# A two-layer transformer trunk: where the token squares stand, and which engine makes three kinds of product

## The chip, the cores and the metric

The kernel runs on one core of a Trainium2 chip. The metric is the device time of one execution in microseconds (us); lower is better. The core has a matrix engine (TensorE, PE in the rows), a vector engine (VectorE, DVE), a scalar engine (ScalarE, ACT), a general engine (GpSimd, POOL) and a sync engine (SyncE, SP) that issues the DMA transfers. Each works through its own list of instructions in the order in which they stand and waits for the others by semaphores.

## What is computed

The reference runs two layers over 512 tokens of width 1024 in float32. A layer is, cut to what matters here:

```
h = rmsnorm(x, g_pre_mix)
proj = h @ w_in                       # q, k, v, index heads of four attention kinds
mix = concat(attention a, b, c, d)    # q, k of a, d and the index heads take rotary tables
x = x + rmsnorm(mix @ w_out, g_post_mix)
h = rmsnorm(x, g_pre_mlp)
m = square(relu(h @ w_up)) @ w_down
x = x + rmsnorm(m, g_post_mlp)
x = x + sigmoid(x @ w_ple_gate) * (p_i @ w_ple_proj)
```

`rmsnorm(x, g)` is x times the reciprocal root of the mean of its squares over the 1024 columns, times g.

## The kernel before

The 512 tokens are four tiles of 128 (`tt` 0 to 3), and a tile's 1024 columns are two halves of 512. The residual x lies in eight tiles named R (128x512). Every float32 matrix product is made of three matmuls: each operand is split into a rounded part and a rest (`whi`, `wlo` for weights, `hth`, `htl` for the transposed activations). The weights come by DMA into `wst` (two buffers), `whi` is a rounded copy and `wlo` the difference; there are five buffers of each.

**The order of the work** is not written by hand. The builder records all operations, with a priority that is the place of recording (moved by `plan.shift`), and a planner then walks through modelled time with fixed costs and writes out each engine's list. An operation recorded with `plan.either` is given to the engine that the planner finds free sooner. `plan.after(i)` holds recorded operations behind operation i in the planner. A named tile such as X, Z or R has a fixed number of buffers (X 4, Z 6, R 19), which are handed to its users in the order of recording; a later user waits until an earlier one is done.

**A layer's start.** `mixing` multiplies each half tile by the gain (`gained_half`: X <- R, Z), transposes it on TensorE and splits it into `hth`, `htl`. The norm's factor is not applied there: `mean_square` squares both halves on ScalarE (with the sum as a second output, `ss`), two small GpSimd operations make the mean, and a GpSimd power makes column tt of `r`. `row_of` transposes the four columns of r (TensorE), ScalarE copies the row into an X tile, and `rope_tables` multiplies sine and cosine by it, into four tiles `tab`. In layer 0 the tables come from `positions`, which a DMA puts into a Z tile, by some twenty VectorE operations and four sines on ScalarE; in layer 1 they are loaded. The first projections, `ik` and the four `iq`, land in the two PSUM buffers `ps_mm`, and leave them by a shuffle and by a product with a table (R <- ps_mm, tab).

**The output projection** (`token_major` with `evac_w` and `done_w`) goes half by half: half 0 is finished for all four tiles (its products with the gain are P <- P, Z), then half 1 tile by tile: ScalarE squares the tile in PSUM, VectorE multiplies by the gain, GpSimd makes the factor, VectorE adds to the residual (two SCALAR_TENSOR_TENSOR, R <- P, ss, R), and then come, for each half, the product with the MLP's gain (X <- R, Z), four transposes, `hth` and `htl`. The MLP's first two tiles (`cut = 2`) are made in column halves, tokens 0 to 255 first. **The MLP's end and the gate** go the same way; the gate's result is sigmoid(PSUM) times `yq`, added to R (`evac_g`), and written to DRAM.

All planned instructions show line L429, the planner's emitting line, in the profile; so they are told apart by their tiles.

Of the kernel before, what the change touches and what calls it, by code (L numbers as in the profile page):

```python
# [14 lines left out]
ALU = mybir.AluOpType  # L15
# [425 lines left out]
class Builder:  # L441
# [77 lines left out]
    def mean_square(self, x, tt, tag):  # L519

        ss = self.tile([128, 4], F32, "ss")
        with self.plan.after(len(self.plan.ops) - 1):
            for i in range(2):
                self.square_half(ss, x[tt][i], i, tag=tag)
        return ss[:, 3:4]

    def add_normed(self, ss, yg, x):
# [409 lines left out]
    def mixing(self, L, x):  # L937
        nc, t = self.nc, self.t
        lam_init = 0.8 - 0.6 * math.exp(-0.3 * L)
        gb = self.gain(t["g1"][L])  # L940
        hT = self.new_hT()
        self.r = self.const([128, 4], "r")
        self.plan.bias = {"DVE": self.gain_bias}
        for tt, i in [(tt, i) for tt in range(4) for i in (0, 1)] if L == 0 else \
                [(tt, i) for i in (0, 1) for tt in range(4)]:
            with self.plan.shift(self.lead[i] if L else 0):
                self.gained_half(x, gb, tt, i, hT, self.hT_tags[(tt, i)[L == 0] % 2], self.first[2 * tt + i] if L == 0 else "vg")
        for tt in range(4):
            ms = self.mean_square(x, tt, "X")
            nc.gpsimd.tensor_tensor(self.r[:, tt:tt + 1], ms, self.mhalf[:, 0:1], op=ALU.pow)  # L950
        if L == 0:
            self.more_constants()
        with self.plan.shift(self.table_shift):
# [57 lines left out]
        def step_mix():  # L1011
# [11 lines left out]
            a=lambda: self.attention_a(r["aq"], r["ak"], r["va"], r["S"]),  # L1023
            b=lambda: self.attention_b(self.decay(zf), r["bq"], r["bk"], r["vb"]),
# [15 lines left out]
    def layer(self, L, x, last):  # L1040
        nc, t = self.nc, self.t
# [32 lines left out]
        x = self.load_x()  # L1074
        gpost = self.gain(t["g2"][L])
        gb = self.gain(t["g3"][L])
        y = [self.tile([128, D], F32, "P4") for tt in range(4)]
        y = [(a[:, :512], a[:, 512:]) for a in y]
        ss = [self.tile([128, 4], F32, "ss4") for tt in range(4)]
        eps4 = [None] * 4  # L1080
        hT = None

        def evac_w(half, tt, ps):
            if (half, tt) in part:
                z = y[tt][half]
                nc.vector.tensor_tensor(z, ps, part[half, tt], op=ALU.add)
                self.square_half(ss[tt], z, half)
                self.plan.either(*[(e, "tensor_tensor", (z, z, gpost[half]), dict(op=ALU.mult))
                                   for e in ("gpsimd", "vector")])
                return  # L1090
            self.square_half(ss[tt], ps, half)
            nc.vector.tensor_tensor(y[tt][half], ps, gpost[half], op=ALU.mult)

        def done_w(tt):
            nonlocal hT
            if hT is None:
                hT = self.new_hT()
            self.add_normed(ss[tt], y[tt], x[tt])


            for i in range(2):
                self.gained_half(x, gb, tt, i, hT, "ps_sc")
            ms = self.mean_square(x, tt, "Z")
            eps4[tt] = self.tile([128, 1], F32, "eps4")
            nc.gpsimd.tensor_scalar(eps4[tt], ms, ms, EPS, op0=ALU.mult, op1=ALU.mult)

        self.token_major(lambda half, i: t["wo"][L, half, self.mixed[i]], [2 * g + k for g in self.mixed for k in (0, 1)],
                         lambda k: (self.mixh[:, k, :], self.mixl[:, k, :]), evac_w, done_w, (False, True), part)

        self.plan.bias = {"DVE": self.mlp_bias}  # L1110
# [54 lines left out]
        def evac_g(half, tt, ps, c=slice(0, 512)):  # L1165
            s = self.tile([128, T], F32, "Z")[:, c]
            nc.scalar.activation(s, ps, AF.Sigmoid)
            xh = x[tt][half][:, c]
            for o, a, b, op in ((s, s, yq[half, tt][:, c], ALU.mult), (xh, xh, s, ALU.add)):
                self.plan.either(*[(e, "tensor_tensor", (o, a, b), dict(op=op)) for e in ("vector", "gpsimd")])  # L1170
            dst = self.out if last else self.xscr
            nc.sync.dma_start(dst[tt * 128:(tt + 1) * 128, half * 512 + c.start:half * 512 + c.stop], xh)

        self.token_major(lambda half, i: t["wg"][L, half, i], range(8),
                         lambda k: (xT[0][:, k, :], xT[1][:, k, :]), evac_g, lambda tt: None, (True, True), fine=last)
        self.xdram = self.xscr
        return x
# [191 lines left out]
```

## Time and profile before

| | |
|---|---|
| median of three runs | 1526.0 us (1525.25 to 1530.46) |
| the profiled execution | 1525.37 us, of which its span is 1523.4 us |
| TensorE busy | 1443.8 us, 95% of the span |
| VectorE, ScalarE, GpSimd busy | 905.1, 659.9, 405.7 us |
| mean granted TensorE clock | 0.985 |

The span goes from the first to the last instruction; the time of an execution holds some 2 us around it. Busy shares are averages over stages that are limited by different things.

### The profile page before, as it was taken

How to read it: one execution, taken by the hardware profiler on the slowest of the kernel's cores; microseconds unless marked ns; L12 is line 12 of the kernel's file. 1: busy time of each engine (PE TensorE's matmuls, PEld its weight loads, DVE VectorE, ACT ScalarE, POOL GpSimd, SP SyncE). 2: the span in 40 equal slices, each digit the busy share in tenths (PEclk: the TensorE clock that was granted, in tenths of full speed). 3: DMA queues.
4: the chain of work that ended last, by engine and by line, in shares of the span. 5: the costliest groups of instructions: out<-in, count | busy, mean ns of one | idle time of the engine just before them, and what ended most of it. 6: DMA issues, size and time to landing. Idle time of an engine off the chain costs nothing.

```text
span 1523.4 us, 19903 instructions
## 1 busy us (share of the span) xinstructions
PE 1443.8 (95%) x7476; PEld 1171.7 (77%) x7476; DVE 905.1 (59%) x1772; ACT 659.9 (43%) x1298; POOL 405.7 (27%) x309
## 2 busy tenths in 40 slices
PE   6899998998999999999979999889989999999998
PEld 6867777777888888887779678667778888888877
DVE  7789998755424333335555999986554243433463
ACT  4266657644423223233343665667443332322331
POOL 4564455354000000002144636463520000000020
PEclk9899999999999999999999999999999999999999
DMA  4321122223222222221421211113132222222221
GB/s 159 99 84 57 63 77 91 77 83 111 92 88 97 97 97 97 94 88 68 131 92 58 83 56 63 63 63 111 49 125 97 97 98 97 90 90 97 97 74 65
DMA packets 44625, 133.91 MB, mean 88 GB/s; under 512 B 6897, under 2 KB 8177, under 8 KB 44529
## 3 DMA queue, kind: packets, MB, share of 16 engines
q1 hardware_dynamic: 44528, 132.64, 26.4%
q8 instruction: 59, 0.97, 0.3%
q14 instruction: 38, 0.30, 0.1%
HBM read 127.38 MB, written 5.24 MB: 87 GB/s over the span
## 4 chain that ended last, share of the span: by engine, by line
PE 67%; DVE 21%; POOL 4%; issue 3%; ACT 3%; DMA 2%; SPq 0%; ACTq 0%; POOLq 0%; DVEq 0%
PE ps_mm L429 25%; PE ps_sc L429 25%; PE ps_tp L429 16%; DVE Z L429 5%; DVE S L429 4%; DVE R L429 3%; DVE m L429 2%; DVE P L429 2%; PE ps_sc L426 2%; POOL ss L429 2%; DVE O L429 1%; POOL X L429 1%; ACT Z L429 1%; DVE htl L429 1%; DMA wst<-in_wq 1%
## 5 line engine op out<-in xcount | busy, mean ns | idle before, releaser
L429 DVE TENSOR_TENSOR wlo<-wst,whi 128x1024 fp32r<-128x1024 f32 x149 | 188.8, 1268 | 348.9 <-ACT whi L429 348.6
L429 ACT ACTIVATE whi<-wst 128x1024 fp32r<-128x1024 f32 (+1 forms) x210 | 220.4, 1051 | 389.5 <-PE ps_tp L429 204.0
L429 POOL TENSOR_TENSOR wlo<-wst,whi 128x1024 fp32r<-128x1024 f32 (+1 forms) x71 | 171.5, 2418 | 164.3 <-ACT whi L429 155.0
L429 PE MATMUL ps_sc<-hth,wlo 128*128 128x512 f32 (+1 forms) x544 | 208.0, 383 | 0.0
L429 PE MATMUL ps_sc<-hth,whi 128*128 128x512 f32 (+1 forms) x544 | 207.9, 382 | 0.0
L429 PE MATMUL ps_sc<-htl,whi 128*128 128x512 f32 (+1 forms) x544 | 207.5, 382 | 0.0
L429 POOL TENSOR_SCALAR ss<-ss,eps 128x1 f32<-128x1 f32 x8 | 3.8, 477 | 652.3 <-ACT Z L429 652.3
L429 PE MATMUL ps_mm<-hth,whi 128*128 128x512 f32 (+1 forms) x400 | 147.8, 371 | 9.5 <-DVE R L429 8.9
L429 PE MATMUL ps_mm<-htl,whi 128*128 128x512 f32 (+1 forms) x400 | 147.8, 370 | 3.4 <-DVE htl L429 3.4
L429 PE MATMUL ps_mm<-hth,wlo 128*128 128x512 f32 (+1 forms) x400 | 146.1, 366 | 0.9 <-DVE wlo L429 0.9
L429 PE MATMUL ps_mm<-whi,htl 128*128 128x512 f32 (+2 forms) x344 | 120.5, 351 | 5.6 <-DVE htl L429 5.6
L429 PE MATMUL ps_mm<-whi,hth 128*128 128x512 f32 (+2 forms) x344 | 121.4, 353 | 0.4 <-DVE V L429 0.4
L429 PE MATMUL ps_mm<-wlo,hth 128*128 128x512 f32 (+2 forms) x344 | 119.8, 349 | 0.1
L429 PEld LDWEIGHTS ps_sc<-htl,whi 128*128 128x128 f32 x544 | 102.9, 189 | 21.5
L429 PEld LDWEIGHTS ps_sc<-hth,wlo 128*128 128x128 f32 x544 | 102.9, 189 | 21.3
L429 PEld LDWEIGHTS ps_sc<-hth,whi 128*128 128x128 f32 x544 | 103.0, 189 | 21.1
L429 ACT ACTIVATE Z<-Z,m 128x256 f32<-128x256 f32 (+3 forms) x160 | 86.2, 541 | 39.3 <-DVE m L429 38.7
L429 PE MATMUL ps_tp<-whi,V 128*128 128x512 f32 x256 | 96.4, 394 | 0.0
L429 PE MATMUL ps_mm<-whi,V 128*128 128x512 f32 x256 | 96.3, 394 | 0.0
L429 PEld LDWEIGHTS ps_mm<-hth,whi 128*128 128x128 f32 x400 | 78.5, 197 | 20.4 <-issue 11.4
L429 PEld LDWEIGHTS ps_mm<-htl,whi 128*128 128x128 f32 x400 | 78.7, 197 | 14.9 <-DVE htl L429 4.0
L429 POOL TENSOR_TENSOR R<-R,R 128x512 fp32r<-128x512 f32 (+1 forms) x56 | 73.0, 1303 | 57.0 <-ACT R L429 46.8
(214 smaller groups left out, 2978.1 us busy)
## 6 DMA issues: line engine op xcount, KB each, us to landing
wst<-in_wu SPq DMA_DIRECT2D x64, 512.0 KB, 3.2
wst<-in_wd SPq DMA_DIRECT2D x64, 512.0 KB, 3.2
wst<-in_wq SPq DMA_DIRECT2D x40, 512.0 KB, 3.6
wst<-in_wo SPq DMA_DIRECT2D x16, 512.0 KB, 3.2
wst<-in_wg SPq DMA_DIRECT2D x16, 512.0 KB, 3.2
R<-in_x SPq DMA_DIRECT2D x16, 256.0 KB, 3.7
Z<-in_g SPq DMA_DIRECT2D x16, 256.0 KB, 3.3
wst<-in_wv SPq DMA_DIRECT2D x8, 512.0 KB, 3.2
```

The lines of the kernel that those rows point to most:

```text
L426: r = nc.tensor.matmul(*[res(v) for v in a], **k)
L429: r = getattr(getattr(nc, eng), fn)(*[res(v) for v in o.a], **{n: res(v) for n, v in o.k.items()})
```

## The change

Three things are changed. `mean_square` no longer holds its squares behind the operation recorded last. In `mixing` each tile's squares and its column of r are recorded right behind that tile's second gained half, inside its shift, and the squares' unused result goes into a Z tile instead of an X tile. And three kinds of operation that the planner could give to GpSimd or VectorE go to VectorE always: the products P <- P, Z of the output projection's half 0, the products X <- R, Z ahead of the MLP, and the product and sum of the gate.

```diff
     def mean_square(self, x, tt, tag):
         ss = self.tile([128, 4], F32, "ss")
-        with self.plan.after(len(self.plan.ops) - 1):
-            for i in range(2):
-                self.square_half(ss, x[tt][i], i, tag=tag)
+        for i in range(2):
+            self.square_half(ss, x[tt][i], i, tag=tag)
         return ss[:, 3:4]
...
                 self.gained_half(x, gb, tt, i, hT, self.hT_tags[(tt, i)[L == 0] % 2], self.first[2 * tt + i] if L == 0 else "vg")
-        for tt in range(4):
-            ms = self.mean_square(x, tt, "X")
-            nc.gpsimd.tensor_tensor(self.r[:, tt:tt + 1], ms, self.mhalf[:, 0:1], op=ALU.pow)
+
+                if i == 1:
+                    ms = self.mean_square(x, tt, "Z")
+                    nc.gpsimd.tensor_tensor(self.r[:, tt:tt + 1], ms, self.mhalf[:, 0:1], op=ALU.pow)
...
                 self.square_half(ss[tt], z, half)
-                self.plan.either(*[(e, "tensor_tensor", (z, z, gpost[half]), dict(op=ALU.mult))
-                                   for e in ("gpsimd", "vector")])
+                nc.vector.tensor_tensor(z, z, gpost[half], op=ALU.mult)
                 return
...
             for i in range(2):
-                self.gained_half(x, gb, tt, i, hT, "ps_sc")
+                self.gained_half(x, gb, tt, i, hT, "ps_sc", "v")
...
             for o, a, b, op in ((s, s, yq[half, tt][:, c], ALU.mult), (xh, xh, s, ALU.add)):
-                self.plan.either(*[(e, "tensor_tensor", (o, a, b), dict(op=op)) for e in ("vector", "gpsimd")])
+                nc.vector.tensor_tensor(o, a, b, op=op)
```

What this does to the engines' lists follows at three places. Numbers behind a name are a buffer's, and each build numbers anew.

SyncE at the program's start, from the second weight load (wst <- in_wq) on; R <- in_x are halves of tiles 2 and 3, Z <- in_pos the positions. Before:

```order
L429 DMA wst_135<-in_wq 128x1024
L429 DMA Z_140<-in_pos 128x512
L429 DMA invf_147<-in_invf 128x3
L429 DMA R_151<-in_x 128x512
L429 DMA R_155<-in_x 128x512
L429 DMA R_166<-in_x 128x512
L429 DMA R_175<-in_x 128x512
L429 DMA bfb_178<-in_bf 128x4
L429 DMA snk_184<-in_sinks 128x4
L429 DMA wst_205<-in_wq 128x1024
```

After:

```order
L429 DMA wst_142<-in_wq 128x1024
L429 DMA invf_149<-in_invf 128x3
L429 DMA R_156<-in_x 128x512
L429 DMA R_160<-in_x 128x512
L429 DMA R_164<-in_x 128x512
L429 DMA R_175<-in_x 128x512
L429 DMA bfb_184<-in_bf 128x4
L429 DMA snk_190<-in_sinks 128x4
L429 DMA wst_220<-in_wq 128x1024
L429 DMA Z_247<-in_pos 128x512
```

The load of the positions has moved from ahead of x's tiles 2 and 3 to behind the third weight load. On ScalarE in the same stretch the eight squares, which stood behind the last `hth` (two of them behind the first two sines), now stand between the `hth`, ahead of all sines.

ScalarE at layer 1's start, from the last `hth` of the transposed tiles (ps_sc) to the copy of r's row (X <- ps_tp); `X,ss<-R` is a square. Before:

```order
L429 ACTIVATE hth_157<-ps_sc_6850 128x4x128
L429 ACTIVATE X_6883,ss_6884<-R_2911 128x512
L429 ACTIVATE X_6891,ss_6884<-R_2951 128x512
L429 ACTIVATE whi_6903<-wst_6854 128x792
L429 ACTIVATE X_6916,ss_6917<-R_3014 128x512
L429 ACTIVATE X_6926,ss_6917<-R_3099 128x512
L429 ACTIVATE X_6955,ss_6956<-R_3119 128x512
L429 ACTIVATE X_6963,ss_6956<-R_3267 128x512
L429 ACTIVATE whi_6970<-wst_6876 128x792
L429 ACTIVATE X_6976,ss_6977<-R_3272 128x512
L429 ACTIVATE X_6980,ss_6977<-R_3282 128x512
L429 ACTIVATE X_6988<-ps_tp_6930 128x512
```

After (seven of the eight squares stand further up, between the sigmoids and `hth`; the last is `Z_6865,ss_6743<-R_3282`):

```order
L429 ACTIVATE whi_6850<-wst_6807 128x1024
L429 ACTIVATE Z_6865,ss_6743<-R_3282 128x512
L429 ACTIVATE whi_6877<-wst_6826 128x1024
L429 ACTIVATE hth_166<-ps_sc_6881 128x4x128
L429 ACTIVATE whi_6930<-wst_6895 128x792
L429 ACTIVATE X_6959<-ps_tp_6949 128x512
```

No square stands behind a `whi` copy of 792 columns any more.

GpSimd in layer 0's output projection, half 1, from tile 2's power (ss <- ss, mhalf) on. Before:

```order
L429 TENSOR_TENSOR ss_824_3684<-ss_824_3684,mhalf_68 128x1
L429 TENSOR_SCALAR ss_3958<-ss_3958 128x1 x2
L429 TENSOR_TENSOR wlo_3976<-wst_3807,whi_3967 128x1024
L429 TENSOR_SCALAR eps_883_3997<-ss_3958 128x1
L429 TENSOR_TENSOR X_4003<-R_3267,Z_3543 128x512
L429 TENSOR_SCALAR ss_825_3741<-ss_825_3741 128x1
L429 TENSOR_TENSOR ss_825_3741<-ss_825_3741,mhalf_68 128x1
L429 TENSOR_TENSOR X_4050<-R_3272,Z_3536 128x512
L429 TENSOR_SCALAR ss_4055<-ss_4055 128x1
L429 TENSOR_TENSOR X_4081<-R_3282,Z_3543 128x512
```

After:

```order
L429 TENSOR_TENSOR ss_824_3684<-ss_824_3684,mhalf_68 128x1
L429 TENSOR_SCALAR ss_3980<-ss_3980 128x1 x2
L429 TENSOR_SCALAR eps_892_4013<-ss_3980 128x1
L429 TENSOR_SCALAR ss_825_3741<-ss_825_3741 128x1
L429 TENSOR_TENSOR ss_825_3741<-ss_825_3741,mhalf_68 128x1
L429 TENSOR_SCALAR ss_4079<-ss_4079 128x1 x2
L429 TENSOR_SCALAR eps_901_4106<-ss_4079 128x1
```

The 512-column products and the 1024-column subtraction have left GpSimd here; VectorE has them, each X pair right behind its tile's two sums. Over the whole program VectorE has 14 products X <- R, Z, four P <- P, Z and two sums R <- R, Z more, and 17 instructions more in all, since the planner gives it a few others less. Outside the two layer starts and the two passages from the output projection to the MLP, the lists of all engines are the same but for single rows.

## Rows read from the trace of the kernel before

**Rows 1.** The page: span, and busy time with share by engine.

```profile
span 1523.4 us, 19903 instructions
PE 1443.8 (95%) x7476; PEld 1171.7 (77%) x7476; DVE 905.1 (59%) x1772; ACT 659.9 (43%) x1298; POOL 405.7 (27%) x309
```

**Rows 2.** Whom TensorE waited for: us in total, times, longest.

```profile
PE ps_sc L429 <- POOL X L429: 13.5, 13, 3.4
...
PE ps_mm L429 <- DVE R L429: 8.9, 2, 5.1
...
PE ps_tp L429 <- POOL r L429: 7.2, 3, 3.4
```

**Rows 3.** Timeline of TensorE, program start: start, us, [idle before <- releaser].

```profile
38.46 0.47 PE L429 MATMUL ps_tp<-ident,r 128*128 128x128 f32 x1 [3.44 <-POOL r L429]
44.00 0.55 PE L429 MATMUL ps_mm<-hth,whi 128*128 128x256 f32 x1 [5.06 <-DVE R L429]
```

**Rows 4.** Timeline of ScalarE, program start.

```profile
34.68 0.61 ACT L429 ACTIVATE X<-R 128x512 f32<-128x512 f32 x1
...
39.03 0.60 ACT L429 ACTIVATE X<-ps_tp 128x512 f32<-128x512 f32 x1 [1.08 <-PE ps_tp L429]
```

**Rows 5.** Timeline of VectorE, program start.

```profile
22.68 3.24 DVE L429 TENSOR_SCALAR Z<-Z 128x512 f32<-128x512 f32 x3
...
32.48 0.68 DVE L429 SCALAR_TENSOR_TENSOR Z<-Z 128x512 f32<-128x512 f32 x1
```

**Rows 6.** Timeline of GpSimd, program start.

```profile
14.19 6.42 POOL L429 TENSOR_TENSOR X<-R,Z 128x512 f32<-128x512 f32 x4 [1.08 <-DVE wlo L429]
22.97 2.66 POOL L429 TENSOR_TENSOR wlo<-wst,whi 128x1024 fp32r<-128x1024 f32 x1 [2.37 <-ACT whi L429]
```

**Rows 7.** Tile Z, first 40 us: its transfer of positions, the table operations, its transfers' landing.

```profile
L429 DVE TENSOR_SCALAR Z<-Z x10: 408/412/2572, 21.4 to 37.3; 128x512 f32<-128x512 f32 x10
...
L429 SPq DMA_DIRECT2D Z<-in_pos x1: 623/623/623, 6.8 to 6.8; - x1
...
DMA to landing us min/median/max: 2.0/4.5/6.7
```

**Rows 8.** Timeline of TensorE, layer 1's start.

```profile
792.57 0.48 PE L429 MATMUL ps_tp<-ident,r 128*128 128x128 f32 x1 [3.36 <-POOL r L429]
796.88 0.55 PE L429 MATMUL ps_mm<-hth,whi 128*128 128x256 f32 x1 [3.83 <-DVE R L429]
```

**Rows 9.** Timeline of ScalarE, layer 1's start.

```profile
789.83 0.61 ACT L429 ACTIVATE X<-R 128x512 f32<-128x512 f32 x1
...
793.14 0.60 ACT L429 ACTIVATE X<-ps_tp 128x512 f32<-128x512 f32 x1 [2.60 <-PE ps_tp L429]
```

**Rows 10.** Timeline of GpSimd, layer 1's start: tile 3's last sum.

```profile
775.85 1.30 POOL L429 TENSOR_TENSOR R<-R,Z 128x512 f32<-128x512 f32 x1 [22.38 <-PE ps_tp L429]
```

**Rows 11.** TensorE by stretch: length, busy us (matmuls in it), granted clock, DMA share, GB/s.

```profile
798.00:800.00 2.00, 2.00 (x11) 0.50 0.04 8
...
804.00:808.00 4.00, 4.00 (x38) 1.00 0.00 0
```

**Rows 12.** TensorE's waits in 327 to 372 us (first row) and 1080 to 1124 us.

```profile
PE ps_sc L429 <- POOL X L429: 5.0, 5, 3.3
PE ps_sc L429 <- POOL X L429: 6.2, 6, 3.4
```

**Rows 13.** Timeline of TensorE, layer 0's passage from output projection to MLP.

```profile
355.11 0.85 PE L429 MATMUL ps_sc<-ident,X 128*128 128x128 f32 x4 [3.33 <-POOL X L429]
...
369.95 0.39 PE L429 MATMUL ps_sc<-hth,whi 128*128 128x512 f32 x1
```

**Rows 14.** Timeline of GpSimd, same passage.

```profile
350.00 3.35 POOL L429 TENSOR_TENSOR wlo<-wst,whi 128x1024 fp32r<-128x1024 f32 x1
```

**Rows 15.** VectorE's groups: xcount | busy us, mean ns of one | idle before.

```profile
L429 DVE TENSOR_TENSOR wlo<-wst,whi 128x1024 fp32r<-128x1024 f32 x149 | 188.8, 1268 | 348.9 <-ACT whi L429 348.6
...
L429 DVE TENSOR_TENSOR X<-R,Z 128x512 f32<-128x512 f32 x10 | 6.9, 688 | 6.2 <-DMA Z<-in_g 4.9 <-POOL R L429 1.2
```

## The prediction, made before the changed kernel ran

> **What bounds the kernel now.** I read the page first: TensorE is busy for 95% of the span [rows 1], so a change to the other engines can only give back time in which TensorE waits, or runs at the lower of its two clocks. The list of TensorE's waits comes second. Its largest entries are the products X <- R, Z made by GpSimd (13.5 us in 13 waits), the rotary products that empty `ps_mm` (8.9 us in two waits) and the column r (7.2 us in three) [rows 2]. The reader is to see that these 29.6 us are exactly what the change touches, and that each comes at few places. Third I read the timeline at those places, which are four: the start of each layer, and the passage from output projection to MLP in each layer. Since the lists of all engines are otherwise nearly the same before and after, I take every other stretch as unchanged, and the sum has four terms.
>
> **Term A, the program's start: 4.8 us less.** TensorE finishes `ik` and the first `iq` and then stands still for 3.44 us, until the last column of r can be transposed at 38.46, and for 5.06 us more until 44.00, when a rotary product has emptied a `ps_mm` [rows 3]. Two chains end there. One is r: tile 3's squares stand on ScalarE behind the first two sines and begin at 34.68, and the copy of r's row begins at 39.03 [rows 4]. The other is the angles: VectorE's last operation ahead of the first sine runs at 32.48 for 0.68 us [rows 5]. Now r is last, by some 4 us.
>
> In the changed order all squares stand between the `hth`, ahead of the sines. GpSimd's six gain products end near 20.6 (14.19 + 6.42) [rows 6]; with two powers and some means between them and one 2.66 us subtraction [rows 6] behind, r is complete near 26. Then the angles decide, and these come later than before. Their load was issued at 6.84 [rows 7]; now it needs a Z buffer that tile 2's square gives up near 16 (tile 2's gain product begins at 14.19 [rows 6], its square follows an `hth`), and landing takes 2.0 to 6.7 us [rows 7], so 18 to 23. From the conversion of the positions to the product that frees `ps_mm`, VectorE's new list has 27 operations: 12 scalar operations and the conversion at 0.41 [rows 7], eight of 0.68 like the one at 32.48 [rows 5], and six others (two `htl`, two shuffles, two products) that I put at 0.69 like a product of that size [rows 15]. That is 5.3 + 5.4 + 4.1 = 14.9 us. From 20 it ends at 35 if nothing holds it.
>
> Something does. Three of these scalar operations took 3.24 us together [rows 5] while a GpSimd subtraction ran [rows 6], against 1.2 at 0.41 each: 2 us lost to one GpSimd operation. Two such subtractions stand in the stretch after the change, so up to 4 us, and `htl` of tile 3 waits for a product that ends near 21.5. I take 39.2 for TensorE's restart, near the upper end because before, too, the operations beside GpSimd were the long ones: 4.8 us gained. The bounds are 36 (nothing held, 8 us gained) and 42 (positions landed at 23, 2 us gained). A pause of several us remains, so I leave the restart at the lower clock as it is.
>
> The Trainium skill, SBUF — State Buffer, section Who interferes with whom, says that a VectorE operation in a two-port mode, or with two SBUF inputs, and a GpSimd operation that reads SBUF shut each other out for a whole instruction. The 3.24 us agree with that. It speaks against the change, which gives VectorE twenty more operations with two SBUF inputs; it is priced below as the third rival.
>
> **Term C, layer 1's start: 9.5 us less.** Here the tables are loaded early and only r is late. The squares stand on ScalarE behind copies of 792 columns that wait for TensorE; the last begins at 789.83, the copy of r's row at 793.14 [rows 9], and TensorE waits 3.36 us for r and 3.83 for the product that frees `ps_mm`, restarting at 796.88 [rows 8]. From the copy's start to the restart it is 3.74 us. In the new order tile 3's last square follows its last sum, which GpSimd began at 775.85 for 1.30 us [rows 10] and VectorE now makes in 0.69; adding a square of 0.61 [rows 9] and some 2 us of means and power, r is there by 781. TensorE's list has the four transposes of r some 3 us of matmuls ahead of the end of `iq` 0, which came at 788.5 (3.36 + some 0.7 before 792.57 [rows 8]), so the copy begins at 786 and `ps_mm` is free at 786 + 3.74 = 789.8. That is 7.1 us earlier, and leaves a pause of 1 us. After the old pause 11 matmuls fell into 2 us at clock 0.50, against 38 into 4 us at 1.00 [rows 11], that is 19 into 2; the low level held for some 5.5 us, so it cost 5.5 x (1 - 11/19) = 2.3 us. After a pause of 1 us I expect full clock. Sum 9.4, taken as 9.5 with the small wait at tile 3; bounds 7 (the clock falls anyway) and 10.5.
>
> **Terms B and D, the two passages to the MLP: 4.2 us less each.** TensorE waits 5.0 us in layer 0 and 6.2 us in layer 1 for X [rows 12]. The longest wait, 3.33 us up to 355.11 [rows 13], is not for arithmetic but for a queue: tile 2's second X stands on GpSimd behind a subtraction that takes 3.35 us from 350.00 [rows 14]. In the new list VectorE makes X at 0.69 [rows 15] right behind the sums, near 350.6. TensorE's two transposes of tile 2 then stand within the output projection's last matmuls, and the MLP's first column halves begin near 352.5 instead of 355.6. They need 48 matmuls, with tile 3's transposes some 6.5 us (38 fall into 4 us at full clock [rows 11], those that reach over an edge included; I count 34): 359. The second column halves need tile 3. Its square, power, sums, X, and both `hth` and `htl` now stand on VectorE among three `wlo` of 1.27 [rows 15]: counting from tile 3's last matmul near 352.3, 0.8 of square, VectorE's backlog of two `htl` and a `wlo` to 354.5, product 0.7, two sums 1.4, two X 1.3, then `htl`, `wlo`, `htl` behind TensorE's transposes, which gives 361.5. Half of a column half, 1.4 us, hangs on that last `htl`, and one whole follows, 2.8: the first full-width matmul begins at 365.7 against 369.95 [rows 13]. That is 4.2 us. If VectorE's queue costs nothing it is 364.6 and 5.3 us; if each of the three `wlo` takes 2.0 instead of 1.27, it is 2.0. Layer 1 runs the same list, and takes the same.
>
> **What lies under cover.** The four products of half 0 and the gate's two sums stand where TensorE has other tiles' matmuls to run, and VectorE is busy for 59% of the span [rows 1]. At 0.69 each they add 4 us of VectorE work; without cover that would be the cost, and I count nothing.
>
> **Sum.** 4.8 + 9.5 + 2 x 4.2 = 22.7 us off the profiled execution's own 1525.37 us gives **1502.7 us**. The median of the runs, 1526.0, is 0.6 above the profiled one, which is inside what one measurement tells. The bounds together are 13 us (1512.4) and 29 us (1496.3).
>
> **Rivals.**
> First, the positions come too late: if they land behind the third weight load and its copies hold VectorE, the angle chain ends where r did before. Its point of decision is a landing at 25; it speaks for this that the load is now behind the squares and a 512 KB transfer, against it that the transfers pause about there. Term A is then nothing: 1507.5.
> Second, VectorE's queue eats the passages: each X pair stands ahead of a `wlo` and of the next tile's `htl`. For it speaks that VectorE then holds sums, X, `htl` and `wlo` of one tile in one row; against it, that four X pairs at 0.69 add only 5.5 us [rows 15] to a passage of some 40. Terms B and D nothing: 1511.1.
> Third, slower: the moved products meet GpSimd's wide operations and are held for a whole one. One such meeting costs some 2 us (the 3.24 against 1.2), and with 14 X, four P and two sums moved, eleven meetings on a path cancel the gain; sixteen, all those in the passages and the gate, would give 1502.7 + 32 = 1535. Against it: GpSimd's list in the passage has only 1-column operations left between the tiles. By the Trainium skill's rule (SBUF — State Buffer, Who interferes with whom) each meeting would cost what is left of GpSimd's operation.
> A case that the change does nothing, since the squares were not what was waited for, is shut out in layer 1 by the rows; in layer 0 it is the first rival.
>
> **How the numbers follow.** I give the forecast 0.62, the first rival 0.15, the second 0.15, the third 0.04, and 0.04 to unseen waits elsewhere. The predicted time is the forecast's. A range of 1495 to 1512 takes in the bounds of the four terms and both milder rivals, and leaves out the third, the unseen, and part of the others' tails. About 0.5% (7.6 us) is what a measurement of this kernel can tell from no change; faster by more than that means under 1518.4. Forecast and two rivals are under it: faster 0.91, same 0.06, slower 0.03.
>
> **What would show it.** After the change TensorE's waits should hold no X by GpSimd in the passages and next to none for r; in layer 1 it should restart near 790 less the time gained before, at full clock; at the start, r's last transpose should run before the first sine and the restart come near 39, with the last wait on VectorE's table operations. The distance from the output projection's last matmul to the first full-width MLP matmul (18.4 us now) should be near 14. I am wrong if the start restarts after 42, if `htl` of tile 3 holds TensorE for over 3 us, or if a new wait appears in the gate or the attention.

## The result, and where the time went

The changed kernel takes 1507.9 us (median of four runs, 1505.6 to 1514.9) against 1527.0 us for the kernel before on the same chip: a ratio of 0.9878, with a 95% interval of 0.9860 to 0.9896. Its profiled execution took 1507.25 us. The forecast was 1502.7 us with a range of 1495 to 1512: the sign and the range held. The profiled executions, from which the forecast was counted, differ by 18.1 us and the medians by 19.1, where 22.7 us were forecast.

The page of the changed kernel, first lines:

```profile
span 1505.5 us, 19889 instructions
PE 1445.8 (96%) x7476; PEld 1173.3 (78%) x7476; DVE 908.8 (60%) x1789; ACT 661.1 (44%) x1299; POOL 376.7 (25%) x291
```

TensorE is busy for as long as before, GpSimd 29 us less, VectorE 4 us more. TensorE's waits (us in total, times, longest):

```profile
PE ps_mm L429 <- DVE R L429: 9.2, 2, 7.9
...
PE ps_mm L429 <- DVE htl L429: 7.4, 3, 2.8
...
PE ps_sc L429 <- POOL X L429: 2.5, 2, 2.2
```

Of the three entries of [rows 2], X by GpSimd is down from 13.5 to 2.5 us, r is gone, and the rotary product is as large as before: its 7.92 us at the program's start take the place of the 3.44 for r and the 5.06 for the product [rows 3].

**Layer 1's start** is what was forecast. Timelines of TensorE, ScalarE and VectorE there:

```profile
780.00 0.27 PE L429 MATMUL ps_tp<-ident,r 128*128 128x128 f32 x1
784.08 0.36 PE L429 MATMUL ps_mm<-hth,whi 128*128 128x256 f32 x1 [1.31 <-DVE R L429]
...
771.73 0.65 ACT L429 ACTIVATE Z<-R 128x512 f32<-128x512 f32 x1
...
780.31 0.60 ACT L429 ACTIVATE X<-ps_tp 128x512 f32<-128x512 f32 x1 [1.69 <-PE ps_tp L429]
...
783.25 0.68 DVE L429 TENSOR_TENSOR R<-ps_mm,tab 128x512 f32<-128x512 f32 x1
```

The last square now begins 8.6 us ahead of the copy of r's row, r's transposes wait for nothing, and a pause of 1.31 us is left of 3.36 and 3.83 [rows 8]. The granted clock in the stretch behind the pause is 1.00 (19 matmuls in 2 us), where it was 0.50 with 11 [rows 11]:

```profile
786.00:788.00 2.00, 2.00 (x19) 2.00 (x19) 1.98 (x3) 0.63 (x1) 0.76 (x1) 1.00 0.20 29
```

**The passage** from the output projection to the MLP in layer 0, on TensorE: the only wait left, and the first full-width MLP matmul.

```profile
359.75 0.39 PE L429 MATMUL ps_sc<-htl,whi 128*128 128x256 f32 x1 [0.52 <-DVE htl L429]
...
363.54 0.39 PE L429 MATMUL ps_sc<-hth,whi 128*128 128x512 f32 x1
```

**The program's start:** TensorE restarts at 40.83 us, not at 39.2. Timelines of TensorE, then VectorE, then GpSimd:

```profile
40.83 0.55 PE L429 MATMUL ps_mm<-hth,whi 128*128 128x256 f32 x1 [7.92 <-DVE R L429]
...
21.22 0.85 DVE L429 CAST Z<-Z 128x512 f32<-128x512 int32 x1
22.73 3.00 DVE L429 TENSOR_SCALAR Z<-Z,invf 128x512 f32<-128x512 f32 x2
...
29.51 4.67 DVE L429 SCALAR_TENSOR_TENSOR Z<-Z,Z 128x512 f32<-128x512 f32 x4
...
22.83 2.62 POOL L429 TENSOR_TENSOR wlo<-wst,whi 128x1024 fp32r<-128x1024 f32 x1
30.41 2.62 POOL L429 TENSOR_TENSOR wlo<-wst,whi 128x1024 fp32r<-128x1024 f32 x1 [3.60 <-ACT whi L429]
```

r is no longer late; the angle chain begins with the conversion at 21.22 and stands still beside both GpSimd subtractions (two scalar operations 3.00 us, four of the others 4.67).

A ledger shows where the time went. For the same matmul in two traces it gives the start before minus the start after, as a median over a stretch of the kernel before's time; the rise from one column to the next is the gain made between them. It is worked out from TensorE's timelines; the other rows are the experiments below, each by one profiled execution.

```
stretch (us of before)   48-56 180-215 280-300 380-440 680-720 820-850 1060-72 1180-1240 1480-1500
changed kernel            2.3    0.2     1.0     6.3     5.6    14.7    13.8    18.6     18.3
squares_only              3.1    1.0     1.8     3.8     3.1    10.4     7.9     9.8      9.5
products_only             2.4    1.2     1.9     3.1     3.1     3.0     3.1     3.4      3.4
layer0_late               2.5    1.3     2.1     7.4     7.4    17.7    15.4    21.0     21.0
mlp_squares_held          2.5    0.3    -1.9    -1.1    -1.8     7.0     5.4     5.1      4.8
products_low_v            0.3    0.3     1.1     7.5     7.5     6.9     8.1    13.4     13.4
after_low_g               3.6    1.5     2.2     4.0     3.3    11.1     8.5    10.7     10.4
before_hth128             2.4    0.6     0.0    -0.2     0.4    -1.0    -5.1    -5.2     -4.9
r_ss_padded_low_v         2.7    2.5     2.0     9.2     9.4    19.3    18.4    25.2     25.2
```

For the changed kernel: passages 5.3 and 4.8 us (forecast 4.2 each), layer 1's start 9.1 (9.5), and of the program's start (4.8) 1.0 us is left at 280. That is 20.2 us; 1.9 us are lost again in stretches that the forecast took as unchanged (0.7 from 380 to 720, 0.9 from 820 to 1072, 0.3 at the end). So the start is 3.8 us short, the passages are 1.7 us better than forecast, and the losses about cancel that. But why the passages gained was not yet known.

A passage's gain by the ledger takes in the output projection ahead of it. The length of the passage alone, from the output projection's last matmul to the first full-width MLP matmul, fell from 18.6 and 18.4 us (layers 0 and 1) to 13.5 and 13.9.

### The profile page after: what moved, and what is told of

It is laid out like the page before. It is cut to its first block, busy times and chain, and to the rows that moved or that the text cites. A ratio compares the mean times of both kernels' runs of the same rounds, so it can differ in the third digit from the quotient of the medians.

```text
span 1505.5 us, 19889 instructions
## 1 busy us (share of the span) xinstructions
PE 1445.8 (96%) x7476; PEld 1173.3 (78%) x7476; DVE 908.8 (60%) x1789; ACT 661.1 (44%) x1299; POOL 376.7 (25%) x291
## 5 line engine op out<-in xcount | busy, mean ns | idle before, releaser
L429 DVE TENSOR_TENSOR wlo<-wst,whi 128x1024 fp32r<-128x1024 f32 x150 | 184.2, 1228 | 355.6 <-ACT whi L429 355.4
L429 POOL TENSOR_TENSOR R<-R,R 128x512 fp32r<-128x512 f32 (+1 forms) x58 | 76.6, 1321 | 59.1 <-ACT R L429 46.0
```

The costliest lines, as they stand in the source:

```text
L429: r = getattr(getattr(nc, eng), fn)(*[res(v) for v in o.a], **{n: res(v) for n, v in o.k.items()})
```

## The experiments

All times are medians beside the kernel before on the same chip; ratios are to it.

### The parts alone

`squares_only` makes the edits of `mean_square` and `mixing` alone, `products_only` the three others alone (with the squares held and placed as before).

> Only the squares stand early; the three kinds of product stay free between VectorE and GpSimd, as before. Theory (the parts add, each where it stands): layer 1's start gains its 9.5 us, the program's start restarts TensorE near 40.8 and keeps some 1 us of that by 300 us, the two passages stay at 18.4 to 18.6 us from the last output-projection matmul to the first full-width MLP matmul. Sum: 10 to 11 us under the kernel before, some 1515. Rival (layer 1's gain needs the gate's sums on VectorE, since GpSimd's last sum of 1.30 us stands ahead of the last square): layer 1's start gains under 7 us and the sum is under 8 us.

1517.1 us, ratio 0.9945 (0.9929 to 0.9961): 9.1 us, 1 to 2 us less than the theory's sum. Layer 1's start gained 7.3 us (3.1 to 10.4) of the changed kernel's 9.1: most of it comes from the squares. The other 1.8 us go with the edits that are left out here (at 749.65 TensorE waits 1.41 us for an X by GpSimd, 0.26 in the changed kernel); which of them was not run alone. Unforeseen: each passage gained 2 us by the ledger, although no product was moved, and its length alone fell to 14.8 us in both layers, where 18.4 to 18.6 were expected; the output projection ahead took some 1.7 us more. With the squares free the planner gave GpSimd no weight subtraction in these passages; before, one stood in each (layer 0's is in [rows 14]).

> Only the three kinds of product go to VectorE; the squares stand as before. Theory (the parts add): both passages fall to some 13.5 us, 5 us each; the program's start restarts TensorE at 44.0 and layer 1's start still waits over 3 us for r and over 3 us for the rotary product. Sum: 10 us under the kernel before, some 1516. Rival (part of the 10 us in the passages came from what stood ahead of them, not from X on VectorE): under 6 us.

1525.1 us, ratio 0.9989 (0.9977 to 1.0001): next to nothing. The passages gained 1.2 and 0.2 us, not 5, and are 19.1 and 19.8 us long. So the passages' gain is no sum of the parts (2.0 + 1.2 against 5.3). Layer 0's passage in `products_only`, on VectorE, GpSimd and TensorE:

```profile
346.43 3.52 DVE L429 SCALAR_TENSOR_TENSOR R<-P,ss,R 128x512 f32<-128x512 f32 x2
...
346.66 2.74 POOL L429 TENSOR_TENSOR wlo<-wst,whi 128x1024 fp32r<-128x1024 f32 x1 [1.20 <-ACT whi L429]
...
350.70 1.23 PE L429 MATMUL ps_sc<-ident,X 128*128 128x128 f32 x8 [2.50 <-DVE X L429]
```

The planner has left GpSimd two subtractions here. Beside one of them tile 2's two sums take 3.52 us, where two such sums take 1.42 us elsewhere in this passage, and TensorE waits 2.50 us for the X behind them: the third rival's mechanism, in the place where the forecast had ruled it out. The Trainium skill, SBUF — State Buffer, section Who interferes with whom, says that a VectorE instruction with two SBUF inputs contends with a GpSimd instruction that reads SBUF, and that the port pair they share is an exclusive lock. The 3.52 us agree with it.

### The start's part undone, and its load moved

`layer0_late` has the squares of layer 0's start as before; `pos_in_V` lets the positions land in another tile:

```diff
-            posi = self.tile([128, T], I32, "Z")
+            posi = self.tile([128, T], I32, "V")
```

> The change without its part in layer 0's start: there the squares stand at the end as before, in X tiles, and the positions load early. Theory (the start's 3.2 us at the restart are nearly all given back by 120 us: a longer stretch at the low clock after the restart, a slower pace of the matmuls, and a fall of the clock near 115): time within 2.5 us of the changed kernel, 1506 to 1510. Rival (the start's gain is kept, and the loss comes later and from elsewhere): 3 us or more above the changed kernel, 1511 or more.

1506.9 us, ratio 0.9876 (0.9859 to 0.9892), the changed kernel's 0.9878: from the change's part in layer 0's start no gain can be told from noise.

> The change, with the positions landing in a V tile, so that their load waits for no square and stands ahead of x's tiles 2 and 3 as before. Theory (the angle chain on VectorE, from the conversion of the positions on, sets TensorE's restart): the conversion runs near 17 instead of 21.2 and the restart comes 3 to 4 us earlier, at 37 to 38; time 1 to 4 us under the changed kernel, by how much of it the clock gives back. Rival (GpSimd's two 1024-column subtractions and the htl between the angle operations set it, not the start of the chain): restart at 40 or later and the time the same within 1 us.

1507.9 us, ratio 0.9878 (0.9865 to 0.9892): the same, and the theory fell. The conversion ran at 16.76, 4.5 us earlier, but the restart came at 40.72. Single operations of the chain beside GpSimd's subtractions now took 2.83 and 2.40 us, two table products beside a third subtraction 2.92 us together, and `htl` stood between the others. The clock fell in this execution too (0.50 in 29 to 31 us), but VectorE was busy without a pause from the conversion to the product that frees `ps_mm`: its own list and the meetings set the restart, as the rival had it.

Why nothing is left is shown by runs whose lists at the start equal the kernel before's word for word on all engines. Granted clock of TensorE in 27 to 31 us, first the kernel before, then `products_only` (length, busy us, matmuls, clock, DMA share, GB/s):

```profile
27.00:29.00 2.00, 2.00 (x15) 0.69 0.55 221
29.00:31.00 2.00, 2.00 (x11) 0.50 0.00 0
```

```profile
27.00:29.00 2.00, 2.00 (x20) 1.00 0.47 188
29.00:31.00 2.00, 2.00 (x19) 1.00 0.00 0
```

```profile
41.98 0.55 PE L429 MATMUL ps_mm<-hth,whi 128*128 128x256 f32 x1 [5.06 <-DVE R L429]
```

The clock fell in one execution and not in the other, and the restart is at 44.00 or 41.98. In the four other runs with these lists it was at 42.01 and 42.04, with the clock at 1.00 in 27 to 31 us, and at 43.53 and 45.07, with 0.50 in 29 to 31; the median over the six is 42.8; in the seven with the change's lists at the start it lay between 39.76 and 41.42, at 40.6 in the median. So the change gains some 2 us at the restart, and the 44.00 of [rows 3] was partly an accident. What it gains is not kept: by 180 us the ledger is down to 0.2.

### Which part makes the passages short

`mlp_squares_held` undoes one line of the change: the hold on the squares ahead of the MLP.

```diff
-            ms = self.mean_square(x, tt, "Z")
+            ms = self.mean_square(x, tt, "Z", True)
```

The added argument makes `mean_square` hold its squares as before, here alone.

> The change, with the squares ahead of the MLP held behind the operation recorded last, as in the kernel before; all else as in the change. Theory (the passages gain only where the products X on VectorE and the free squares come together, since with held squares the planner gives two weight subtractions of 1024 columns back to GpSimd): the passages lengthen from 13.5 to 17 or 18.5 us each, time 7 to 10 us above the changed kernel, near 1516. Rival (the products alone make the passages short, and the run with the products alone lost its gain through its late squares in the layers' starts): passages stay under 15 us, time within 2 us of the changed kernel.

1519.0 us, ratio 0.9947 (0.9930 to 0.9963): this one line is worth 10.5 us by the ratios. The passages gained 0.8 and -0.3 us, and from the last output-projection matmul to the first full-width one it is 19.1 and 20.1 us. GpSimd again has two subtractions in each passage, and TensorE a like wait, 2.47 us, for tile 2's X:

```profile
354.68 1.23 PE L429 MATMUL ps_sc<-ident,X 128*128 128x128 f32 x8 [2.47 <-DVE X L429]
```

The next two set GpSimd's subtractions by hand: `products_low_v` takes them out of the passages of `products_only`, `after_low_g` puts two into those of the changed kernel.

```diff
-    def wload(self, src, S):
+    def wload(self, src, S, low="vg"):
...
# products_low_v
-            wh, wl = self.wload(t["wu"][L, f], 1024)
+            wh, wl = self.wload(t["wu"][L, f], 1024, "v" if f < 4 else "vg")
-            ws = [self.wload(src(half, i), 1024) for i in range(4)]
+            ws = [self.wload(src(half, i), 1024, "v" if part and half else "vg") for i in range(4)]
# after_low_g
-            wh, wl = self.wload(t["wu"][L, f], 1024)
+            wh, wl = self.wload(t["wu"][L, f], 1024, "g" if f < 2 else "vg")
```

> The run with the products alone, with the weight subtractions wlo of the output projection's half 1 and of the MLP's first four tiles given to VectorE always, so that GpSimd has none in the passages. Theory (in the run with the products alone VectorE's sums and X stood still beside GpSimd's subtractions, two sums taking 3.52 us instead of 1.42): the passages come down to 14 to 15 us, time 7 to 10 us under the kernel before. Rival (it is the held squares on ScalarE ahead of hth that keep the passages long): passages of 17 us or more, time less than 4 us under the kernel before.

1513.9 us, ratio 0.9917 (0.9897 to 0.9936): 12.5 us under the kernel before, with late squares at all places. The passages came to 15.7 and 15.6 us, somewhat more than expected, and the output projection ahead of them ran faster as well: output projection and passage together gained 6.4 and 5.3 us (1.1 to 7.5, and 8.1 to 13.4). Tile 2's two sums on VectorE, and TensorE's waits for X and for `htl`:

```profile
345.37 1.41 DVE L429 SCALAR_TENSOR_TENSOR R<-P,ss,R 128x512 f32<-128x512 f32 x2
...
347.53 1.23 PE L429 MATMUL ps_sc<-ident,X 128*128 128x128 f32 x8 [0.38 <-DVE X L429]
...
350.44 0.38 PE L429 MATMUL ps_sc<-hth,whi 128*128 128x256 f32 x1 [1.68 <-DVE htl L429]
```

The sums take 1.41 us instead of 3.52. The wait for `htl` is left, and with the squares held the passages stay some 2 us longer than the changed kernel's.

> The change, with the weight subtractions wlo of the MLP's first two tiles given to GpSimd always. Theory (a GpSimd subtraction beside VectorE's sums and X costs the passage some 2 us each): the passages lengthen to 16 to 18 us and the time is 5 to 9 us above the changed kernel. Rival (VectorE has slack there, and the subtraction that it loses gives back what the meetings cost): passages within 1 us of 13.5 and the time the same within 2 us.

1514.4 us, ratio 0.9914 (0.9897 to 0.9932): two more subtractions by GpSimd at each passage cost 6.5 us over the changed kernel (5.5 by the ratios), as expected, but at another place. From the last output-projection matmul on nothing changed (13.3 and 13.5 us); the loss is ahead of it. VectorE, GpSimd and TensorE:

```profile
345.64 3.47 DVE L429 TENSOR_TENSOR X<-R,Z 128x512 f32<-128x512 f32 x2
...
345.14 2.83 POOL L429 TENSOR_TENSOR wlo<-wst,whi 128x1024 fp32r<-128x1024 f32 x1 [0.86 <-ACT whi L429]
...
348.66 0.95 PE L429 MATMUL ps_sc<-ident,X 128*128 128x128 f32 x4 [2.18 <-DVE X L429]
```

Tile 2's X pair takes 3.47 us, against 1.29 for the other pairs, TensorE waits those 2.18 us, and behind the wait the clock is down (0.50 in 350 to 352 us). The other subtraction, from 331.86 on, met nothing that was waited for.

### The pace of the matmuls, and better versions

In the ledger the changed kernel loses 0.7 us from 380 to 720, within the MLP where nothing was changed, and after the restart it falls back further. Both losses, the 0.7 us and some 2 us from 48 to 215, are in every run told so far with early squares in layer 0; with late squares the first is in none and the second is 1.2 us or nothing. TensorE's windows show it at full clock, first the changed kernel, then `products_only`:

```profile
54.00:58.00 4.00, 4.00 (x35) 1.00 0.43 126
```

```profile
54.00:58.00 4.00, 4.00 (x38) 1.00 0.19 76
```

By the starts of 24 matmuls, eight of 256 columns take 0.96 us here and 0.91 there. The DMA share differs as well (0.43 and 0.19), so traffic is a rival here; the best version below rules it out. Memory is given out in the order of first use. With r used early, `hth` and `htl` begin at byte 7136 and 23520 of a partition instead of 7104 and 23488, and `whi` moves too.

```diff
-        self.r = self.const([128, 4], "r")
+        self.r = self.const([128, 16], "r")
```

> The change with the tile r made 16 columns wide instead of 4. The change makes r before hth and htl, so these begin at byte 7136 and 23520 of a partition, not multiples of 64, where the kernel before and the two runs with late squares in layer 0 have 7104 and 23488; with 16 columns they begin at 7168 and 23552, multiples of 64 again, and nothing else moves against a multiple of 64. Theory (the slower pace of the matmuls in the change comes from where hth and htl lie): eight 256-column matmuls after the first restart take 0.90 us again instead of 0.96, the drift of 1.2 us against the kernel before over layer 0's MLP and of 0.4 us over layer 1's is gone; 2 to 2.5 us under the changed kernel. Rival (the pace comes from the places of whi, wlo or V, or from the memory traffic): 0.96 again and the same time.

1504.5 us, ratio 0.9848 (0.9826 to 0.9870), 3.5 us under the changed kernel's median, by ratios whose intervals overlap. Eight matmuls took 0.94 us, a third of the way back, not the 0.90 of the theory. In layer 0's MLP the ledger now rises by 0.8 us where it fell by 0.7.

> The kernel before with one small tile made 20 columns wide instead of 4, which moves hth and htl from byte 7104 and 23488 to 7168 and 23552 (a multiple of 128 instead of 64 more than one) and every other large tile by a multiple of 128; each engine's list is the same. Theory (the pace of TensorE's matmuls depends on where hth and htl lie): as in the run with r padded, against which the kernel before drifted by 0.9 us over layer 0's MLP and 1.4 us over layer 1's, it is 2 to 3 us under the kernel before. Rival (that drift came with whi, wlo or V, which lay elsewhere in that run): no drift, the same time.

1530.5 us, ratio 1.0025 (1.0014 to 1.0035): slower, against theory and rival. The MLPs did run faster (0.6 us from 380 to 720, 0.3 us in layer 1's), but eight matmuls at the start took 0.95 instead of 0.91 us, and between 680 and 1072 the clock fell more often: 5.5 us lost. So `hth` and `htl` alone do not set the pace.

> The change, with the weight subtractions of the output projection's half 1 and of the MLP's first four tiles given to VectorE always. With the products alone this gained 10 us. Theory (in the change GpSimd has two subtractions left ahead of the passages, in the output projection, beside which VectorE's sums run long; in the passages it has none): the passages stay at 13.5 us, and the output projection gives 1 to 3 us in each layer: 2 to 6 us under the changed kernel, 1502 to 1506. Rival (VectorE's queue becomes the bound): passages over 14.5 us and the same time or more.

1505.0 us, ratio 0.9857 (0.9839 to 0.9875): 3 us under the changed kernel, by ratios whose intervals overlap. The passages stayed at 13.4 and 13.8 us.

> The run before this one, with r 16 and each ss 32 columns wide, so that hth and htl begin at a multiple of 128 and whi, wlo and V at a multiple of 64. Theory (the two gains add): 3 to 5 us under the run before this one, near 1500; eight 256-column matmuls after the first restart in 0.91 us. Rival (only hth and htl matter): 0.94 us as with r padded alone, and 3 us under it.

1499.6 us (1499.3 to 1500.0), ratio 0.9819 (0.9806 to 0.9832): the best version, 27 us under the kernel before and clear of the changed kernel's interval. It is also clear of the interval of `after_low_v`, whose lists are the same on all engines: the 5.4 us between the two come with the places of the tiles alone. By one profile of each, part of that is the clock, which fell near 113 us in `after_low_v` and not here. Eight matmuls take 0.91 us again, at a DMA share (0.42) like the changed kernel's, so the traffic does not make the slower pace:

```profile
54.00:58.00 4.00, 4.00 (x37) 1.00 0.42 131
```

> The change without its part in layer 0's start, with the weight subtractions on VectorE as in the other two and hth and htl at a multiple of 128. Theory (layer 0's part of the change is worth nothing): within 2 us of the run with r and ss padded, near 1500. Rival (early squares in layer 0 are worth 1.2 us or more once the tiles lie well): 2 to 4 us above it.

1502.4 us, ratio 0.9839 (0.9820 to 0.9858): 2.7 us above the best version, as the rival had it, but the intervals overlap, and its profiled start was the one at 45.07. Its tiles also lie otherwise than in the best version, at the places of `before_hth128`, and eight matmuls take 0.95 us, not 0.91. Whether layer 0's early squares are worth something once the tiles lie well stays open.

## Why the prediction held, and where it did not

**Term C** (9.5 us) was right by its own steps: r was there ahead of the end of `iq` 0, the copy ran at 780.31 (forecast 786, less 5.6 gained before, 780.4), the pause was 1.31 us against 1, the clock stayed up; 9.1 us measured.

**Terms B and D** (4.2 us each) came out at 5.3 and 4.8, inside or at the end of their bounds of 2 and 5.3: `htl` of tile 3 held TensorE for 0.52 us where 1.1 were counted (365.7 against 364.6 us for the first full-width matmul). The size was near and the reason incomplete. The forecast gave the gain to X on VectorE. Alone, that edit gains next to nothing (`products_only`); with the hold on the squares put back the changed kernel loses its passages (`mlp_squares_held`); and with GpSimd's subtractions given to VectorE by hand the products gain without it (`products_low_v`). What shortens the passages is that GpSimd makes no weight subtraction beside VectorE's sums and X: none stands in those of 13.3 to 15.7 us (the changed kernel, `squares_only`, `layer0_late`, `products_low_v`, `after_low_v`), two in those of 19.1 to 20.1 (`products_only`, `mlp_squares_held`). The change brought that about through the planner, which gave the subtractions to VectorE once the squares were free; why its costs tip that way was not traced. The forecast had read the outcome off the new list and so got the time right.

**Term A** (4.8 us) is the term that failed. By the forecast, "I take 39.2 for TensorE's restart" against 44.00. The chain was named rightly (angles, not r), and its end mis-sized by 1.6 us: the conversion ran at 21.2 instead of 20, and the stretch from it to the product that frees `ps_mm` (ending near 40.65) took 19.4 us instead of 18.9 (14.9 and 4 of standing still). The larger error was the 44.00: the same lists restarted at 42 where the clock did not fall at 27 to 31. That leaves some 2 us; of this the slower pace takes 0.7 us by 62 us. In the changed kernel's profile the clock also fell near 115 (0.50 in 116 to 118), which cost 1.3 us against the profile of before; it fell there in `products_only` and `layer0_late` too, so the early squares are not its cause. With the start undone the time is the same within the noise.

That the sum came within 4.6 us of the profiled execution is in part luck: what the passages gave beyond the forecast (1.7 us) made up for losses elsewhere (1.9 us).

**The first rival** (positions too late) did not occur: they were converted at 21.2 us, ahead of its point of decision at 25. Its time, 1507.5, is near the measured one for other reasons. **The second** (VectorE's queue eats the passages) did not occur either: the queue held TensorE for 0.52 us in layer 0 and no longer in layer 1. **The third** (meetings with GpSimd) was rightly ruled out for the changed passages, and is the price of three variants nearby (`products_only`, `mlp_squares_held`, `after_low_g`): 2.1 to 2.2 us for a pair of operations that meets one subtraction.

**Unseen by the forecast**: the pace of the matmuls, some 0.7 us in layer 0's MLP and 0.7 us after the restart; and that the clock's falls differ between executions of the same lists.

## What to carry to other kernels

When a planner places work, an edit's gain may belong to what the planner does elsewhere because of it: run each part alone and look at which wide operations stand on the engine next to the path. A wide GpSimd operation beside a chain of VectorE operations cost this kernel some 2 us per meeting that TensorE waited for, more than the operation would have cost on VectorE (1.2 us). And before a wait is priced from one profile, look at the granted clock ahead of it: at the start some 2 us of the forecast gain of 5 were the clock of that one execution.

## What the runs showed of the hardware that was not expected

The pace of back-to-back matmuls at granted clock 1.00 depends on where their operands lie. Eight of 256 columns after the first restart took 0.91 us with `hth` 64 and `whi` 0 bytes beyond a multiple of 128 (the kernel before and `products_only`), 0.91 with 0 and 64 (`r_ss_padded_low_v`), 0.95 with 0 and 0 (`before_hth128`, `layer0_late_low_v`), 0.94 with 0 and a mixture of 0, 64 and 96 (`r_padded`), 0.96 with 96 and a mixture of 0, 32 and 64 (the changed kernel). The MLP ranks them otherwise: it ran faster with 0 and 0 than with 64 and 0. Which operand counts, and why, stays open; at the start it is worth up to 6% of the pace, and between two versions with the same lists (`after_low_v` and `r_ss_padded_low_v`) the places went with 5.4 us of the whole.

The clock also falls at one place in one execution and not in another of the same lists (27 to 31 us above: down in three of six), which moves single executions by some 2 us at a time; the scatter of the changed kernel's four runs, 9 us, is wider than most of the differences discussed here.
